# Expert weights asked for only after the second block, with the stage's own buffers first in the ring

## The chip, the cores and the metric

The kernel runs on one core of a Trainium2 chip. The metric is the device time of one execution in microseconds (us), median of 3 runs. The engines are TensorE (PE; PEld is its weight load), VectorE (DVE), ScalarE (ACT), GpSimd (POOL) and SyncE (SP). SP issues all DMAs of this kernel, in one queue and in the order of the program.

## The reference, cut to what matters

A first block of two layers works on 256 tokens of width 1024. A second block mixes a state-space branch (s5), a sparse attention and a memory attention, and ends in an output projection:

```python
merged = g_s * (y_ssm @ w_up_ssm) + g_d * (y_dsa @ w_up_dsa) + g_m * (y_mem @ w_up_mem)
x = x + merged @ w_out
x = x + hier_moe(rms_norm_2(x, g_ffn), w_group, b_group, w_expert, b_expert, w_gate, w_up, w_down)
```

`hier_moe` has 32 experts. A router (`w_group`, `w_expert`) picks two of them for each token. Gate, up and down weights of all 32 are read: each expert has 1024x512 gate, 1024x512 up and 512x1024 down, in fp32, 201 MB together.

## The kernel before

The experts run in 16 pairs. Each pair takes 24 pieces of weights of 128x1024 fp32, 512 KB each: 16 of gate and up, then 8 of down, 384 pieces in all. `fetch` (L1330) issues the DMA of the next piece on SP. It takes its buffer from `ring` (L1313), and a manual dependency keeps the pieces in their order of use on the queue. The first lap goes through the 35 letters of `RING` (L42), each one buffer: `e` two tiles of their own (`we`), `u` general tiles of the pool with 16 buffers that both blocks and the experts use (`unit`, L270), `x` four tiles of the pool `wx`, which lies where the second block's working tiles were, `w`, `h`, `l` the buffers of the split projection weights (`wraw`, `whi`, `wlo`), `T`, `t` those of transposed activations (`Thi`, `Tlo`), `b` one row buffer. Four more `u` tiles (`FIRST`) follow, then the laps repeat over the 35.

A piece's DMA waits on SP until the last user of its buffer is done, and everything behind it on SP waits with it. It also waits for one of eight completion semaphores (DMAHW0 to 7), which go round, so at most eight DMAs are under way.

Before the experts stands the second block. Its steps run in the order of the table `ORDER2` (L108 to 113), by `run_steps`. A step `name,args/k` sets `share`; a step without `/k` sets it back to the usual 4. The steps named here: `b,q,i` and `end,q` are the s5 blocks (L931 to L959), `glu` a projection behind them, `up,i,c` the three up projections (`up,0` is the last, w_up_ssm), `ahead,n` calls `fetch` n times. `ahead,2` at the top takes the two `we`; `ahead,6` at the end takes the six `u`.

Behind the table comes the output projection: the transposes (`tsplit`, L286 to L288), then `proj_tok` over eight weight pieces of w_out. Every projection weight is split by `wsplit` (L214): ACT makes `whi` (L216), and `wlo` (L217) comes from POOL for every `share`-th piece, otherwise from DVE:

```python
(G if share[0] and scount[0] % share[0] == 0 else V).tensor_sub(
```

`router_weights` (L1366) loads w_group and w_expert into a `u` tile, scales them (L1374) and splits them into a second `u` tile `wrs` (L1376, L1377). The first steps of the expert stage are the router: transposes of x, sixteen matmuls of `Thi` and `Tlo` with `wrs` (through L149), then some 6 us of small DVE work, then the one-hot gather (L1509) and the experts' matmuls, L1550 (gate, up) and L1572 (down). The program is ordered by a scheduler that follows data, buffers and priorities.

Of the kernel before, what the change touches and what calls it, by code (L numbers as in the profile page):

```python
# [38 lines left out]
HPR = 600  # L39

CAP = 64
RING = "e" * 2 + "u" * 6 + "x" * 4 + "w" * 5 + "h" * 5 + "l" * 4 + "T" * 4 + "t" * 4 + "b"  # L42

FIRST = 4

# [63 lines left out]
ahead,2 mn sa sp lo wm nt kv prep,0 u/6 b,0,1/1 keys/6 vk mem_q sel,0 queries/3 mem,0 b,0,0/3 gate,2,1/6 mem,1 b,0,3/1  # L109
gate,2,0/0 prep,1 up,2,0 up,2,1/0 b,1,0 sel,1 b,0,2/0 b,1,1/1 end,0 dsa,0 dsa,1 gate,1,1/0 b,1,2/2 b,1,3/1  # L110
prep,2 gate,1,0 up,1,0/6 up,1,1/3 b,2,0 end,1 prep,3 b,2,2/2 b,3,0 b,3,2 b,2,1/1 b,2,3/1 gate,0,1 gate,0,0
b,3,1/1 end,2 b,3,3/0 end,3 glu/2 up,0,1/2 up,0,0/2 ahead,6
"""
TWO_PI = 6.283185

# [6 lines left out]
def tile_model(ctx: ExitStack, tc: tile.TileContext, I: dict, out: bass.AP):  # L122
# [1190 lines left out]
    def ring():  # L1313

        n = turns[0]
        turns[0] += 1
        if n < len(RING):
            w = kinds[RING[n]]()
            slots.append(w)
            return w  # L1320
        if n < len(RING) + FIRST:
            return firsts.pop(0)
        return slots[(n - FIRST) % len(RING)]

# [413 lines left out]
```

## Time and profile before

| | |
|---|---|
| median of 3 runs | 1797.05 us (1796.57 to 1798.23) |
| the profiled execution | 1801.36 us, its span 1799.6 us |
| PE busy | 94%, mean granted clock 0.973 |
| DVE, ACT, POOL busy | 57%, 39%, 18% |
| DMA | 389.65 MB, 217 GB/s over the span, about 409 GB/s in the expert stage |
| first and second layer, second block | up to about 1318 us |
| experts | the rest, 1318 to 1799.6 us |

All times below are us from the start of the span of that one execution. PE's 94% is the busy share of pipelined matmuls, and does not say by itself that PE is the limit in the expert stage; the chain of waits and the DMA rate do.

### The profile page before, as it was taken

How to read it: one execution, taken by the hardware profiler on the slowest of the kernel's cores; microseconds unless marked ns; L12 is line 12 of the kernel's file. 1: busy time of each engine (PE TensorE's matmuls, PEld its weight loads, DVE VectorE, ACT ScalarE, POOL GpSimd, SP SyncE). 2: the span in 40 equal slices, each digit the busy share in tenths (PEclk: the TensorE clock that was granted, in tenths of full speed). 3: DMA queues.
4: the chain of work that ended last, by engine and by line, in shares of the span. 5: the costliest groups of instructions: out<-in, count | busy, mean ns of one | idle time of the engine just before them, and what ended most of it. 6: DMA issues, size and time to landing. Idle time of an engine off the chain costs nothing.

```text
span 1799.6 us, 24178 instructions
## 1 busy us (share of the span) xinstructions
PE 1688.6 (94%) x9005; PEld 1266.1 (70%) x9005; DVE 1025.9 (57%) x1659; ACT 708.2 (39%) x1345; POOL 318.4 (18%) x247
## 2 busy tenths in 40 slices
PE   7999999999999999999998998876879999999998
PEld 6899888888798999888877876765644444434342
DVE  6656656666673568675669899799631212212121
ACT  4455555644444656565546552421411010100000
POOL 0111106220102101321024343365100000000000
PEclk9999999999999999999999998987989999999999
DMA  8654445455566534453664633223699999999997
GB/s 261 188 142 137 140 145 144 148 166 164 164 174 178 171 111 141 135 164 102 197 190 149 180 106 111 66 70 107 196 378 369 410 409 408 409 409 409 409 409 297
DMA packets 186104, 389.65 MB, mean 217 GB/s; under 512 B 28736, under 2 KB 66816, under 8 KB 185984
## 3 DMA queue, kind: packets, MB, share of 16 engines
q1 hardware_dynamic: 185984, 388.08, 63.3%
q8 instruction: 72, 1.18, 0.3%
q14 instruction: 48, 0.39, 0.1%
HBM read 386.98 MB, written 1.05 MB: 216 GB/s over the span
## 4 chain that ended last, share of the span: by engine, by line
PE 70%; DMA 13%; DVE 11%; issue 2%; POOL 2%; ACT 1%; SPq 0%; DVEq 0%; POOLq 0%; ACTq 0%
PE proj L149 45%; PE proj L1550 7%; PE sc L149 5%; PE pv L149 4%; PE sc L1572 4%; DMA whi<-in_w_up_dram 2%; DMA Tlo<-in_w_up_dram 2%; DVE wlo L217 2%; PE tp L1509 1%; PE tp L365 1%; PE tp L286 1%; DMA wlo<-in_w_up_dram 1%; DMA wx<-in_w_up_dram 1%; DMA wraw<-in_w_down_dram 1%; DVE u L935 1%
## 5 line engine op out<-in xcount | busy, mean ns | idle before, releaser
L216 ACT CAST whi<-wraw 128x1024 fp32r<-128x1024 f32 x336 | 351.8, 1051 | 319.0 <-PE proj L149 263.1
L217 DVE TENSOR_TENSOR wlo<-wraw,whi 128x1024 fp32r<-128x1024 f32 (+1 forms) x287 | 376.7, 1316 | 172.0 <-PE proj L149 119.2
L149 PE MATMUL proj<-wlo,Thi 128*128 128x512 f32 (+1 forms) x1056 | 419.4, 397 | 6.2 <-DVE wlo L217 6.2
L149 PE MATMUL proj<-whi,Thi 128*128 128x512 f32 (+1 forms) x1056 | 419.4, 399 | 2.3 <-ACT P L988 1.0
L149 PE MATMUL proj<-whi,Tlo 128*128 128x512 f32 (+1 forms) x1056 | 415.7, 396 | 2.4 <-DVE Tlo L288 2.4
L149 PEld LDWEIGHTS proj<-wlo,Thi 128*128 128x128 f32 x1056 | 201.3, 191 | 48.3 <-DVE wlo L217 8.0
L149 PEld LDWEIGHTS proj<-whi,Thi 128*128 128x128 f32 x1056 | 201.4, 191 | 44.6 <-DVE u L1273 1.9
L149 PEld LDWEIGHTS proj<-whi,Tlo 128*128 128x128 f32 x1056 | 200.9, 190 | 43.1 <-DVE Tlo L288 2.9
L217 POOL TENSOR_TENSOR wlo<-wraw,whi 128x1024 fp32r<-128x1024 f32 (+1 forms) x49 | 125.4, 2559 | 434.4 <-PE proj L149 332.4
L149 PE MATMUL proj<-Thi,whi 128*128 128x256 f32 x576 | 165.2, 291 | 6.0 <-DVE u L468 3.0
L149 PE MATMUL proj<-Thi,wlo 128*128 128x256 f32 x576 | 165.8, 289 | 3.6 <-DVE wlo L217 3.6
L149 PE MATMUL proj<-Tlo,whi 128*128 128x256 f32 x576 | 164.8, 290 | 0.1
L1554 DVE SCALAR_TENSOR_TENSOR th<-th,cg,proj 128x512 f32<-128x512 f32 x16 | 12.0, 747 | 214.1 <-PE proj L1550 212.0
L149 PEld LDWEIGHTS proj<-Thi,whi 128*128 128x128 f32 x576 | 112.5, 197 | 7.8 <-DVE u L468 3.2
L149 PEld LDWEIGHTS proj<-Thi,wlo 128*128 128x128 f32 x576 | 113.5, 197 | 4.0 <-DVE wlo L217 3.8
L149 PEld LDWEIGHTS proj<-Tlo,whi 128*128 128x128 f32 x576 | 112.6, 197 | 0.4 <-DVE Tlo L959 0.3
L149 PE MATMUL sc<-u 128*128 128x256 f32 (+1 forms) x416 | 101.0, 359 | 11.8 <-DVE u L930 11.8
L1553 ACT ACTIVATE th<-proj,cg 128x512 f32<-128x512 f32 x16 | 11.0, 687 | 192.4 <-PE proj L1550 192.4
L149 PEld LDWEIGHTS sc<-u 128*128 128x128 f32 x416 | 70.6, 198 | 20.0 <-issue 11.9
L1576 DVE TENSOR_TENSOR u<-sc,u 128x512 fp32r<-128x512 f32 x32 | 22.0, 692 | 109.5 <-ACT u L1575 90.4
L356 ACT ACTIVATE P<-sc,nm 128x256 f32<-128x256 f32 (+1 forms) x152 | 63.7, 432 | 36.2 <-DVE nm L349 22.1
L1575 ACT CAST u<-sc 128x512 fp32r<-128x512 f32 x32 | 18.6, 585 | 136.1 <-PE sc L1572 122.0
(464 smaller groups left out, 2489.1 us busy)
## 6 DMA issues: line engine op xcount, KB each, us to landing
wraw<-in_w_in_dram SPq DMA_DIRECT2D x236, 512.0 KB, 3.8
wraw<-in_w_proj_dram SPq DMA_DIRECT2D x48, 512.0 KB, 4.3
u<-in_w_up_dram SPq DMA_DIRECT2D x25, 512.0 KB, 10.2
wraw<-in_w_out_dram SPq DMA_DIRECT2D x24, 512.0 KB, 4.4
u<-in_w_gate_dram SPq DMA_DIRECT2D x24, 512.0 KB, 10.2
wraw<-in_w_up_dram SPq DMA_DIRECT2D x21, 512.0 KB, 10.2
whi<-in_w_down_dram SPq DMA_DIRECT2D x21, 512.0 KB, 10.2
u<-in_w_down_dram SPq DMA_DIRECT2D x21, 512.0 KB, 10.1
```

Of the source, the lines that this page charges most:

```text
L149: T.matmul(o, l, r, start=start, stop=stop)
L216: S.copy(hi[:, :, :n], raw[:, :, :n])
L217: (G if share[0] and scount[0] % share[0] == 0 else V).tensor_sub(lo[:, :, :n], raw[:, :, :n], hi[:, :, :n].bitcast(F32))
L286: T.transpose(ps[:, b, :], src[:, b * 128:(b + 1) * 128], ident)
L356: S.activation(P[:, i * nS:(i + 1) * nS], scv[:, i, :], AF.Exp, bias=nm[:, i:i + 1], accum_out=l_out[:, i:i + 1])
L365: T.transpose(tp[:, j, :], P[:, j * 128:(j + 1) * 128], ident)
L935: V.tensor_tensor_scan(m[:, 256:512], rb, hi, 0.0, op0=OP.mult, op1=OP.add)
L1509: pin(T.matmul(tp[:, k, :], src[t][:, k0 + k, :], ohv[:, t], start=n == 0, stop=n == 3))
L1550: pin(T.matmul(ps[r], xk, w[:, 512 * j:512 * j + 512], start=k == 0, stop=k == 7))
L1572: pin(T.matmul(po[c][r], hT[:, k, r], w[:, 512 * c:512 * c + 512], start=k == 0, stop=k == 3))
L1575: S.copy(yh[:, c], po[c])
L1576: V.tensor_sub(yl[:, c], po[c], yh[:, c].bitcast(F32))
```

## The change

The step `ahead,6` at the end of `ORDER2` is gone, so no piece beyond the first two is asked for inside the second block. In `RING` the four `x` stand before the six `u`. Pieces 3 to 6 now go to `wx`, pieces 7 to 12 to `u` tiles, which are allocated only in the expert stage, behind the router's own tiles. Since the table now ends with `up,0,0/2`, `share` stays 2 and not 4 for the eight w_out pieces behind it: four of their `wlo` are made on POOL instead of two.

```diff
-RING = "e" * 2 + "u" * 6 + "x" * 4 + "w" * 5 + "h" * 5 + "l" * 4 + "T" * 4 + "t" * 4 + "b"
+RING = "e" * 2 + "x" * 4 + "u" * 6 + "w" * 5 + "h" * 5 + "l" * 4 + "T" * 4 + "t" * 4 + "b"
...
-b,3,1/1 end,2 b,3,3/0 end,3 glu/2 up,0,1/2 up,0,0/2 ahead,6
+b,3,1/1 end,2 b,3,3/0 end,3 glu/2 up,0,1/2 up,0,0/2
```

SP before, from the last w_out load on (`wraw_11799`), where ring pieces 13 to 16 follow directly; all six `u` pieces stand at least 13 rows further up:

```order
L1338 DMA wx_12115<-in_w_up_2_dram 128x1024 [waits DMAHW1_49]
L1338 DMA wx_12117<-in_w_up_2_dram 128x1024 [waits DMAHW2_49]
L201 DMA wraw_11793<-in_w_out_2_dram 128x2x512 [waits DMAHW3_49,DVE_49]
L201 DMA wraw_11799<-in_w_out_2_dram 128x2x512 [waits DMAHW4_49,DVE_49]
L1338 DMA wraw_12155<-in_w_gate_2_dram 128x1024 [waits DMAHW5_49,Pool_49]
L1338 DMA wraw_12157<-in_w_gate_2_dram 128x1024 [waits DMAHW6_49,DVE_49,Activation_49]
L1338 DMA wraw_12163<-in_w_up_2_dram 128x1024 [waits DMAHW7_49,DVE_49]
L1338 DMA wraw_12165<-in_w_up_2_dram 128x1024 [waits DMAHW3_49,DMAHW0_49,DVE_49]
```

SP now, from the last two w_out loads on:

```order
L201 DMA wraw_11781<-in_w_out_2_dram 128x2x512 [waits DMAHW5_49,Pool_49]
L201 DMA wraw_11787<-in_w_out_2_dram 128x2x512 [waits DMAHW6_49,DVE_49]
L1338 DMA u_12088<-in_w_up_2_dram 128x1024 [waits DMAHW7_49,PE_49]
L1338 DMA u_12090<-in_w_up_2_dram 128x1024 [waits DMAHW0_49]
L1338 DMA u_12107<-in_w_gate_2_dram 128x1024 [waits DMAHW1_49,PE_49]
L1338 DMA u_12109<-in_w_gate_2_dram 128x1024 [waits DMAHW2_49,DVE_49]
L1338 DMA u_12115<-in_w_up_2_dram 128x1024 [waits DMAHW3_49,PE_49]
L1338 DMA u_12117<-in_w_up_2_dram 128x1024 [waits DMAHW4_49,PE_49]
L1338 DMA wraw_12155<-in_w_gate_2_dram 128x1024 [waits DMAHW5_49,Pool_49]
L1338 DMA wraw_12157<-in_w_gate_2_dram 128x1024 [waits DMAHW6_49,DVE_49,Activation_49]
```

The six `u` pieces stand between the last w_out load and the rest of the ring. The sixth, `u_12117`, has the address of `u_11851`, which is `wrs`; the PE count that it waits for is that of the last router matmul that reads `wrs` (`proj_11935<-Thi_11896,u_11851`). Before, the first piece that waited for the same matmul was the 30th of the ring:

```order
L1336 DMA wlo_12209<-in_w_down_2_dram 128x1024 [waits DMAHW0_49]
L1338 DMA wlo_12226<-in_w_gate_2_dram 128x1024 [waits DMAHW1_49]
L1338 DMA wlo_12228<-in_w_gate_2_dram 128x1024 [waits DMAHW2_49]
L1338 DMA Thi_12234<-in_w_up_2_dram 128x1024 [waits DMAHW3_49]
L1338 DMA Thi_12236<-in_w_up_2_dram 128x1024 [waits DMAHW4_49]
L1338 DMA Thi_12242<-in_w_gate_2_dram 128x1024 [waits DMAHW5_49,DVE_49,PE_49]
L1338 DMA Thi_12244<-in_w_gate_2_dram 128x1024 [waits DMAHW6_49,DVE_49,PE_49]
L1338 DMA Tlo_12250<-in_w_up_2_dram 128x1024 [waits DMAHW7_49]
```

That is `Thi_12244`, whose buffer was the router's own operand. Now it is the twelfth.

DVE at the last two s5 blocks, before (-) and now (+); L936 to L940 and L950 to L959 are the s5 steps:

```order
 L952 TENSOR_TENSOR cva<-u 128x256
+L1374 TENSOR_TENSOR u<-u,g_11848 128x288
 L936 TENSOR_TENSOR u<-u 128x512
 L937 TENSOR_TENSOR u<-u 128x512
 L953 TENSOR_SCALAR cva<-cva 128x256
+L1377 TENSOR_TENSOR u<-u 128x8x36
 L939 TENSOR_TENSOR u<-u 128x256
 L940 TENSOR_TENSOR u<-u 128x256
 L954 TENSOR_TENSOR cva<-cva,u 128x256
+L950 SCALAR_TENSOR_TENSOR u<-u,s5d,pv 128x256
 L956 SCALAR_TENSOR_TENSOR u<-cva,u 128x256
-L950 SCALAR_TENSOR_TENSOR u<-u,s5d,pv 128x256
```

The two steps on the router's weights moved up into the last s5 block, since their loads now stand ahead of w_out's, and L950 stands before the L956 of the block ahead.

## Rows read from the trace of the kernel before

**Rows 1.** The page: GB/s moved in 40 slices of 45 us.

```profile
GB/s 261 188 142 137 140 145 144 148 166 164 164 174 178 171 111 141 135 164 102 197 190 149 180 106 111 66 70 107 196 378 369 410 409 408 409 409 409 409 409 297
```

**Rows 2.** Busy time by stretch; the first line names the columns.

```profile
core 0: us, PE busy (x) PEld busy (x) DVE busy (x) ACT busy (x) POOL busy (x), PEclk, DMA share, GB/s
...
1248.00:1264.00 16.00, 10.61 (x42) 8.82 (x42) 13.83 (x26) 1.67 (x4) 4.71 (x3) 0.79 0.95 330
1264.00:1284.00 20.00, 17.59 (x79) 13.77 (x79) 14.64 (x23) 10.48 (x18) 5.77 (x17) 0.91 0.65 220
1284.00:1296.00 12.00, 9.80 (x41) 8.09 (x42) 6.13 (x9) 2.54 (x5) 0.10 (x1) 0.86 0.28 91
1296.00:1318.20 22.20, 18.91 (x95) 15.23 (x93) 12.11 (x18) 10.64 (x17) 3.11 (x2) 0.96 0.82 265
1318.20:1352.00 33.80, 25.06 (x114) 12.40 (x114) 10.82 (x54) 3.55 (x7) 0.00 (x0) 0.77 1.03 410
1352.00:1364.00 12.00, 10.38 (x50) 3.77 (x50) 0.75 (x1) 0.58 (x1) 0.00 (x0) 1.00 1.00 349
...
1384.00:1392.00 8.00, 8.00 (x40) 2.75 (x38) 1.38 (x2) 1.17 (x2) 0.00 (x0) 1.00 0.86 265
```

**Rows 3.** SP's queue in order of time: start, length, what, count.

```profile
1248.57 1.13 SPq L1338 DMA_DIRECT2D u<-in_w_up_dram  x2
...
1277.55 7.80 SPq L201 DMA_DIRECT2D wraw<-in_w_out_dram  x2
1285.45 11.37 SPq L1338 DMA_DIRECT2D wraw<-in_w_gate_dram  x2
...
1318.20 0.33 SPq L1338 DMA_DIRECT2D Thi<-in_w_gate_dram  x1
...
1774.23 4.17 SPq L1336 DMA_DIRECT2D Thi<-in_w_down_dram  x4
```

**Rows 4.** Timeline of PE: the last router matmul.

```profile
1317.76 0.41 PE L149 MATMUL proj<-Thi,u 128*72 128x256 f32 x1
```

**Rows 5.** The chain that ended last: start, length, what, two of its links.

```profile
1550.81 10.18 DMA Thi<-in_w_up_dram
...
1643.63 10.18 DMA Tlo<-in_w_up_dram
```

**Rows 6.** The page, DMA issues: count, size, median us to landing.

```profile
wraw<-in_w_in_dram SPq DMA_DIRECT2D x236, 512.0 KB, 3.8
```

**Rows 7.** Timeline of DVE at the end of the s5 blocks and behind it.

```profile
1258.25 0.42 DVE L940 TENSOR_TENSOR u<-u 128x256 f32<-128x256 f32 x1
...
1259.48 0.43 DVE L956 SCALAR_TENSOR_TENSOR u<-cva,u 128x256 f32<-128x256 f32 x1 [0.48 <-ACT cva L955]
1260.56 0.48 DVE L950 SCALAR_TENSOR_TENSOR u<-u,s5d,pv 128x256 f32<-128x256 f32 x1 [0.66 <-PE pv L149]
...
1271.44 0.45 DVE L1374 TENSOR_TENSOR u<-u,g 128x288 f32<-128x288 f32 x1
...
1273.61 0.45 DVE L1377 TENSOR_TENSOR u<-u 128x288 fp32r<-128x288 f32 x1
```

**Rows 8.** Splits of w_out on DVE and POOL, and PE's wait behind them.

```profile
1281.28 2.59 POOL L217 TENSOR_TENSOR wlo<-wraw,whi 128x1024 fp32r<-128x1024 f32 x1
...
1281.55 3.40 DVE L217 TENSOR_TENSOR wlo<-wraw,whi 128x1024 fp32r<-128x1024 f32 x1
...
1295.19 1.23 DVE L217 TENSOR_TENSOR wlo<-wraw,whi 128x1024 fp32r<-128x1024 f32 x1 [0.67 <-PE proj L149]
...
1286.20 0.79 PE L149 MATMUL proj<-whi,Tlo 128*128 128x512 f32 x1 [2.44 <-DVE Tlo L288]
```

**Rows 9.** Timeline of PE: first matmuls of pair 0 on pieces in `wx` and `wraw`.

```profile
1342.38 3.65 PE L1550 MATMUL proj<-wx,u 128*64 128x512 f32 x16 [0.78 <-DVE u L1510]
...
1348.68 3.65 PE L1550 MATMUL proj<-wraw,u 128*64 128x512 f32 x16
```

## The prediction

> **What bounds the kernel now.** I read the page's bytes by slice first [rows 1]. From slice 30 on the rate stands at 408 to 410 GB/s until the last slice: the expert stage ends when its stream of 384 pieces ends. The chain of waits says the same from another side: in the second half it runs through DMAs, one link being a piece from issue to landing (10.18 us), after which the eighth piece behind it is issued [rows 5]. From 1550.81 to 1643.63 there are nine such links, so 92.82 us / 72 pieces = 1.289 us per piece. What happens to the time is therefore decided by one question: how many pieces are already under way when the stream can run without a break, and when that is.
>
> Then I followed SP's queue back to the start of the stream [rows 3]. Six `u` pieces go out from 1248.57 on. The last w_out load leaves just before 1285.45, the next ring pieces wait for `wraw` buffers, and from 1296 to 1318.2 the queue already moves 265 GB/s [rows 2]. The 30th piece (`Thi`) goes out at 1318.20 [rows 3], in the instant in which the last router matmul ends (1317.76 + 0.41 = 1318.17) [rows 4]. So 29 pieces were issued before the router was done. Nothing after that holds the stream for long: two dips, 349 GB/s over 12 us and 265 over 8 us, when the ring is full and PE must free buffers [rows 2].
>
> **The change part by part.** *The new wait.* The six `u` pieces now stand behind the last w_out load. Five of them find free tiles; the stretch 1284 to 1296 has room for them (91 GB/s, DMA share 0.28) [rows 2]. The sixth, piece 12, has the buffer of the router's split weights and waits for the router's last matmul. SP is one queue, and in it all other pieces stand behind piece 12: the `wraw`, `whi` and `wlo` pieces, the first of which went out from 1285.45 to 1315 before, are held too. Where 29 pieces were out at the router's end, 11 will be. That is 18 pieces of 1.289 us, 23 us of stream, of which a part was under way and not landed, and a part was lost again in the two dips. I don't sum these; I time the end of the stream directly.
>
> Call T the time at which the router's last matmul ends. Piece 12 is issued at T. It goes into an empty queue, and lands after the median of such a load, 3.8 us [rows 6]. Seven more are issued right behind it, and piece 20 when piece 12 has landed. From there one piece follows every 1.289 us. The first of the last four `Thi` pieces is the 381st, 361 behind the 20th: T + 3.8 + 361 x 1.289 = T + 469.1. Before it was issued at 1774.23 [rows 3]. The page gives 3.8 for a 512 KB load. The Trainium skill, "DMA: Bandwidth & Descriptors", section "Anatomy of one DMA", fits 2.0 us + bytes / 436 GB/s for the other issue path, an estimate of 3.2 us here; by it the sum would be 0.6 us less, and no run here shows that figure.
>
> With T unchanged at 1318.17 the 381st goes out at 1787.3, 13.0 us later than before. The tail behind it does not change: eight down pieces, their matmuls, the scatter and the store. PE is no hindrance at the start of the stage: the last of pair 0's gate and up pieces, the 16th, lands at about T + 3.8 + 4 x 1.289 = 1327, and PE came to the `wraw` pieces only at 1348.68 [rows 9]. The dips fall away, since the ring is no longer full at that time; they are in the old 1774.23 and not in the new sum, so their gain is already counted.
>
> *What moves T.* Before T stand the end of the s5 blocks, glu, w_up_ssm and w_out.
> (a) L1374 and L1377 move from behind the s5 blocks into the last one, 0.45 us each [rows 7]. DVE has no gap there up to L940, and PE waits for that result, so 0.9 us is added. In their old places nobody waited for them.
> (b) L956 of the third block now comes after L950 of the fourth; its 0.43 us was hidden in DVE's wait for PE, and is now in front of the fourth's chain [rows 7]: +0.4.
> (c) The w_out loads no longer share the DMA with six `u` pieces (330 GB/s from 1248 to 1264) [rows 2]. In the list of waits no engine waits for a w_out piece there, so this gives 0.
> (d) Four splits on POOL and not two. A POOL split is 2.59 us, and a DVE split that ran beside it took 3.40 us, against 1.23 us for one without a neighbour [rows 8]. The first such pair, at 1281, exists before and now, and PE waits 2.44 us behind it both times. The second half of w_out gets one more pair; there PE runs from 1286 on nearly without a gap, and the splits come well ahead of their matmuls. I take 0; uncovered it would be 3.40 - 1.23 = 2.2.
> T = 1318.2 + 0.9 + 0.4 = 1319.5.
>
> T has two ends. Early: the wait of 2.44 us goes, and with it the lower clock behind it, an estimate from the row for 1284 to 1296 of 9.80 x (1 - 0.86) = 1.4 us [rows 2, 8]; T = 1318.2 - 3.8 = 1314.4. Late: (a), (b) and an uncovered (d); T = 1319.5 + 2.2 = 1321.7.
>
> *The sum.* 381st piece at 1319.5 + 469.1 = 1788.6; before 1774.23; the span grows by 14.4 us, from 1799.6 to 1814.0. The profiled execution took 1801.36 us, 4.3 above the median of the runs. I add the difference to the median: 1797.05 + 14.4 = **1811.4 us**, 0.8% slower.
>
> **The rivals.**
> *Not slower: the wait does not bind.* The place is piece 12 on SP. If its buffer were free with the other five, all six would go out in the gap from 1284 to 1296, where 0.72 x 12 = 8.6 us of DMA time lies idle for 6 x 1.289 = 7.7 us of pieces, and the ring would go on as before, with w_out's loads earlier. The price would be about nothing, 1797. The point from which it decides: T + 469.1 = 1774.23, so piece 12 must leave before 1305.1. For this speaks the gap that is there. Against it: the wait in the built program names the router's matmul, the 30th piece, which waited for the same one, went out in the very instant that it ended [rows 3, 4], and T can't come 13 us sooner: PE's idle time from 1264 to 1318.2 is only 2.4 + 2.2 + 3.3 = 7.9 us [rows 2]. Chance 0.08, 0.05 of it within 0.2% and 0.03 faster.
> *Slower, but less.* PE's wait before the w_out matmuls goes since DVE's order changed around it; T = 1314.4, the 381st at 1783.5, 1797.05 + 9.3 = 1806.3. For it: POOL takes the second w_out split, which stood on DVE ahead of the last sums of the up projection. Against it: the pair that made the wait is still there. Chance 0.12.
> *Slower by more: DVE and POOL hold each other up.* The row shows a DVE split 2.2 us longer beside a POOL split [rows 8]. If the added pair has no cover, T = 1321.7 and the time is 1813.6. The Trainium skill, "SBUF — State Buffer", section "SBUF: two separate sides", says that DVE with two SBUF inputs and a reading GpSimd operation exclude each other for a whole instruction; the row agrees, since 1281.28 + 2.59 + 1.23 = 1285.1 is near the DVE split's end at 1284.95. Chance 0.10, since PE had slack there.
> *The forecast*, T near 1319.5 and a stream of 1.289 us per piece: 0.70.
>
> **How the numbers follow.** A difference of 0.2% (3.6 us) is about what a measurement of this kernel can tell from no change. Forecast 0.70, less 0.12, more 0.10: slower 0.92; same 0.05; faster 0.03. The price of a piece has an end of its own: links of 10.18 us without the small gaps between some of them give about 1.28, which takes off 361 x 0.009 = 3.3 us. The range goes from the early T (1806.3) less some of that, 1805.0, to the late T (1813.6) and the 1.7 us by which the runs of before differ, 1815.3. It leaves out the rival in which the wait does not bind.
>
> **What would show it.** In the profile after: the SP queue issues five `u` pieces between about 1285 and 1292 and the sixth right behind the last router matmul, with `wraw<-in_w_gate` behind it; the DMA rate from 1296 to T near zero, then 410 GB/s with no dips near 1352 and 1384; the chain of waits turning to DMAs earlier in the expert stage than before; the last four `Thi` issues near 1788.6; the router's end near 1319.5. If piece 12 leaves before the router ends, or the rate between 1296 and 1318 stays at 265 GB/s, the prediction is wrong at its root. If T lies outside 1314 to 1322, the sum is off by that much, and in particular by (a), (b) or (d).

## The result

The changed kernel takes 1806.53 us (median of 5 runs, 1804.39 to 1807.44) beside 1797.05 for the one before (5 runs, 1795.76 to 1798.23): 9.5 us more, ratio 1.0052, 95% interval 1.0037 to 1.0067. It is slower, as forecast, by 9.5 us and not by 14.4.

The mechanism that the prediction names is there. SP's queue in the changed kernel (start, length, what; the answer to [rows 3]):

```profile
1277.38 0.90 SPq L1338 DMA_DIRECT2D u<-in_w_up_dram  x2
1278.36 1.67 SPq L1338 DMA_DIRECT2D u<-in_w_gate_dram  x2
1282.15 26.31 SPq L1338 DMA_DIRECT2D u<-in_w_up_dram  x2
1308.55 0.86 SPq L1338 DMA_DIRECT2D wraw<-in_w_gate_dram  x2
...
1778.32 4.17 SPq L1336 DMA_DIRECT2D Thi<-in_w_down_dram  x4
```

Five `u` pieces go out up to 1282.15. The row "x2" of 26.31 us holds the fifth and the sixth: the sixth, the 12th piece of the ring, leaves at 1308.13 (1282.15 + 26.31 less the 0.33 of its own issue), and the `wraw` pieces stand behind it. The router's last matmul in the changed kernel ends at 1307.82 + 0.28 = 1308.10:

```profile
1307.82 0.28 PE L149 MATMUL proj<-Thi,u 128*72 128x256 f32 x1
```

The stretches show the same silence (columns and order as in [rows 2], cut at the matching places):

```profile
1243.20:1259.20 16.00, 10.31 (x41) 8.69 (x41) 14.28 (x27) 2.10 (x5) 5.29 (x11) 0.79 0.62 169
1259.20:1279.20 20.00, 17.40 (x83) 13.32 (x84) 15.47 (x23) 10.21 (x17) 8.47 (x11) 1.00 0.59 204
1279.20:1291.20 12.00, 12.00 (x60) 10.01 (x60) 7.73 (x8) 6.37 (x9) 3.07 (x2) 1.00 0.65 245
1291.20:1308.10 16.90, 13.64 (x73) 10.98 (x71) 8.52 (x15) 6.81 (x12) 3.32 (x2) 1.00 0.00 0
1308.10:1339.00 30.90, 22.13 (x105) 11.65 (x106) 10.63 (x53) 2.31 (x6) 0.00 (x0) 0.78 0.98 375
1339.00:1380.00 41.00, 38.69 (x200) 16.64 (x198) 8.72 (x20) 6.08 (x11) 0.00 (x0) 1.00 1.03 409
```

In the 16.9 us before the router's end nothing moves, where it was 265 GB/s. Behind it the queue first fills (375 GB/s over 31 us), and then there is no dip any more: 409 GB/s from 1339 on. In the page's slices (45 us each, against [rows 1]) the row is flat from there to the last:

```profile
GB/s 270 193 137 146 126 162 128 140 187 160 145 198 191 148 120 126 135 175 101 210 196 140 171 104 104 47 83 105 122 387 409 409 409 409 409 409 409 409 409 298
```

The chain of waits turns to the transfers at 1452.90, where it was 1540.60 before, with the same link as in [rows 5]:

```profile
1449.40 3.50 PE sc L1572 x15
1452.90 10.15 DMA whi<-in_w_up_dram
```

**Reading the two traces side by side.** The profiled spans differ by only 5.0 us (1799.6 and 1804.6), less than the medians. The code up to the s5 blocks is the same in both, and yet the same instructions stand 4.6 us apart at 50 us (53.57 and 48.96) and 4.8 us apart at 1215. DVE before, a line of the start and one ahead of the changed stretch:

```profile
53.57 1.00 DVE L511 SCALAR_TENSOR_TENSOR cva<-proj,cw,cva 128x255 f32<-128x255 f32 x2 [1.66 <-ACT cva L509]
...
1218.79 0.68 DVE L929 TENSOR_TENSOR u<-sc,u 128x512 f32<-128x512 f32 x1
```

DVE after, the same two:

```profile
48.96 1.00 DVE L511 SCALAR_TENSOR_TENSOR cva<-proj,cw,cva 128x255 f32<-128x255 f32 x2 [0.22 <-ACT cva L509]
...
1214.01 0.68 DVE L929 TENSOR_TENSOR u<-sc,u 128x512 f32<-128x512 f32 x1
```

So the profiled execution of before had lost 4.6 us within its first 55 us, where the two programs are the same, and 4.8 us ahead of the changed stretch. It is the odd one: in the seven traces of the experiments below the first line stands between 48.7 and 50.7 us, the second between 1211.7 and 1213.6. It fits that this execution took 4.3 us more than the median of its kernel. Below, "aligned" means a time of before less 4.8. Aligned, the effect of the change on the span is 1804.6 - (1799.6 - 4.8) = 9.8 us, as the medians say. It splits into three: the router's end, T, comes at 1308.13 instead of 1318.2 - 4.8 = 1313.4, **5.3 us earlier**; from T to the 381st piece it takes 1778.32 - 1308.13 = 470.2 instead of 1774.23 - 1318.2 = 456.0, **14.2 us longer**; the tail takes 26.3 instead of 25.4, 0.9 longer. -5.3 + 14.2 + 0.9 = 9.8.

### The profile page after: what moved, and what is told of

It is laid out like the page before. It is cut to its first block, busy times and chain, and to the rows that moved or that the text cites. A ratio compares the mean times of both kernels' runs of the same rounds, so it can differ in the third digit from the quotient of the medians.

```text
span 1804.6 us, 24172 instructions
## 1 busy us (share of the span) xinstructions
PE 1695.5 (94%) x9005; PEld 1262.8 (70%) x9005; DVE 1025.9 (57%) x1657; ACT 708.5 (39%) x1345; POOL 323.9 (18%) x249
## 4 chain that ended last, share of the span: by engine, by line
PE 67%; DMA 17%; DVE 10%; POOL 2%; issue 2%; ACT 1%; SPq 0%; DVEq 0%; POOLq 0%; ACTq 0%
PE proj L149 46%; PE sc L149 5%; PE proj L1550 4%; PE pv L149 4%; DMA whi<-in_w_up_dram 3%; DMA u<-in_w_up_dram 3%; PE sc L1572 3%; DVE wlo L217 2%; DMA wraw<-in_w_down_dram 2%; DMA Tlo<-in_w_up_dram 2%; PE tp L365 1%; PE tp L286 1%; DMA wraw<-in_w_up_dram 1%; DMA wlo<-in_w_up_dram 1%; DMA Thi<-in_w_up_dram 1%
## 5 line engine op out<-in xcount | busy, mean ns | idle before, releaser
L217 POOL TENSOR_TENSOR wlo<-wraw,whi 128x1024 fp32r<-128x1024 f32 (+1 forms) x51 | 131.8, 2585 | 424.2 <-PE proj L149 308.0
L149 PEld LDWEIGHTS sc<-u 128*128 128x128 f32 x416 | 70.2, 197 | 22.4 <-issue 14.4
```

Source lines behind the costliest of these rows:

```text
L149: T.matmul(o, l, r, start=start, stop=stop)
```

## The experiments

Two questions were left: is the held piece the whole loss, and does the number of pieces behind it set its size; and why does the router end 5.3 us earlier, where I forecast 1.3 later. All times are medians; experiments 1 to 4 ran beside runs of before with a median of 1795.39 us (29 runs), 5 to 7 beside 1795.69 (17 runs). The ratios are not the quotients of these medians but lie up to 0.14% above them, so a difference to the kernel before is known to within some 2.5 us. Differences below are those of the medians.

| run | us | ratio to before, 95% |
|---|---|---|
| 1: changed, ring in the old order | 1790.97 | 0.9985 (0.9973 to 0.9998) |
| 2: changed, five `u` pieces | 1792.07 | 0.9990 (0.9979 to 1.0000) |
| 3: changed, share of splits as elsewhere | 1806.64 | 1.0074 (1.0057 to 1.0092) |
| 4: before, share of splits as in the changed one | 1795.34 | 1.0002 (0.9989 to 1.0015) |
| 5: before, `ones` without a load | 1790.61 | 0.9977 (0.9967 to 0.9988) |
| 6: changed, held piece is the 17th | 1798.60 | 1.0030 (1.0017 to 1.0043) |
| 7: changed, held piece is the 10th | 1809.27 | 1.0082 (1.0068 to 1.0097) |

**1. Only the early request is taken away.**

```diff
-RING = "e" * 2 + "x" * 4 + "u" * 6 + "w" * 5 + "h" * 5 + "l" * 4 + "T" * 4 + "t" * 4 + "b"
+RING = "e" * 2 + "u" * 6 + "x" * 4 + "w" * 5 + "h" * 5 + "l" * 4 + "T" * 4 + "t" * 4 + "b"
```

(- is the changed kernel.)

> The changed kernel with the ring in its old order (u pieces before the wx pieces); only the six early pieces are left out. In this order the gather's second operand, and not a u piece, gets the buffer of the router's split weights, so no piece of the ring waits for the router before the first Thi piece that needs the router's halves, the 30th. Main theory (the whole loss is the 12th piece waiting on SP for the router's last matmul): nothing but the order on SP's queue differs from the changed kernel; 29 pieces are out when the router ends, as before the change, and the router ends 5.3 us earlier than before as in the changed kernel (1318.2 - 4.8 against 1308.1, times aligned), so 1797.05 - 5.3 = about 1792 us, and at most 1797. Rival (what costs is that the six pieces are asked for later, behind w_out's loads): as the changed kernel, 1806.5 us.

Measured 1790.97 us, 15.6 less than the changed kernel (15.7 less than experiment 3, which ran beside it and has the changed ring) and 4.4 less than the one before (2.7 by the ratio). SP's queue in this run:

```profile
1281.38 1.70 SPq L1338 DMA_DIRECT2D wx<-in_w_up_dram  x2
1284.13 1.63 SPq L1338 DMA_DIRECT2D wraw<-in_w_gate_dram  x2
...
1304.63 1.73 SPq L1338 DMA_DIRECT2D Thi<-in_w_gate_dram  x2
...
1759.90 4.18 SPq L1336 DMA_DIRECT2D Thi<-in_w_down_dram  x4
```

All six `u` pieces, the `wx` and the `wraw` go out before the router ends; the 30th piece, the second of the `Thi` row, leaves at 1306.03 and is again the one that waits for it (the last router matmul ends at 1306.00). From there to the 381st it takes 1759.90 - 1306.03 = 453.9 us, where it was 456.0 before the change. So the half of the change that asks for nothing ahead costs nothing. The loss comes from the other half, the `wx` pieces in front: they shift the rotation of the `u` buffers by one, and give a ring piece the buffer of the router's weights that otherwise the gather takes. In the built program of this run the address of `wrs` (`u_11851`) goes to the gather's `u_12096`; in the changed kernel it goes to `u_12117`, the sixth `u` piece.

**2. The held piece alone is taken away.**

```diff
-RING = "e" * 2 + "x" * 4 + "u" * 6 + "w" * 5 + "h" * 5 + "l" * 4 + "T" * 4 + "t" * 4 + "b"
+RING = "e" * 2 + "x" * 4 + "u" * 5 + "w" * 5 + "h" * 5 + "l" * 4 + "T" * 4 + "t" * 4 + "b"
```

> The changed kernel, order of the ring kept, with five u pieces instead of six, so that the piece which waited for the router's split weights is not there; the ring is one piece shorter. Main theory: 27 to 28 pieces are out at the router's end instead of 11, no silence on the DMA queue before 1308, the 381st piece is no later than about 1771 in the times of the changed kernel, total about 1792 + at most 1.3 us for the slot that is missing when the ring is full = 1792 to 1794 us. Rival (a later request for the ring as such, or wx ahead of u as such): 1806 us or more.

Measured 1792.07 us. `wx` stays in front, 28 pieces are out when the router ends at 1308.16, and the loss is gone all the same. It is 1.1 us above experiment 1; I expected up to 1.3 for the missing slot, but the intervals of the two ratios overlap, so this part is not settled.

**3 and 4. The share of splits.** The last step of the order table sets the share that w_out inherits. Without the `ahead,6` one split in two goes to POOL, with it one in four. Experiment 3 sets the changed kernel back to one in four, experiment 4 gives the kernel before one in two.

```diff
-b,3,1/1 end,2 b,3,3/0 end,3 glu/2 up,0,1/2 up,0,0/2
+b,3,1/1 end,2 b,3,3/0 end,3 glu/2 up,0,1/2 up,0,0/2 ahead,0
```

```diff
-b,3,1/1 end,2 b,3,3/0 end,3 glu/2 up,0,1/2 up,0,0/2 ahead,6
+b,3,1/1 end,2 b,3,3/0 end,3 glu/2 up,0,1/2 up,0,0/2 ahead,6/2
```

> The changed kernel with the share of weight splits that go to POOL in w_out set back to one in four, as the usual share is; before it was one in two only because the last step of the order table sets it. Two of w_out's splits on POOL and not four; nothing else differs. The router ended 5.3 us earlier in the changed kernel than in the one before, where I had forecast 1.3 later. Theory A (it is the splits: with four on POOL the DVE queue ahead of w_out is shorter and PE's wait of 2.44 us goes): PE waits again for a DVE split before w_out, the router ends 3.8 to 6.6 us later, 1810 to 1813 us. Theory B (the early router comes from the order around the s5 blocks, or from the DMA queue free of ring pieces): 1806.5 us within 1.

> The kernel before, with one in two of w_out's splits on POOL instead of one in four; the six early pieces and the ring's order stay. Theory A (the splits on POOL bring the early router): the router ends 3.8 to 5.3 us earlier, and since 29 pieces are out at that time the stream of the experts begins and ends as much earlier: 1792 to 1793 us. Theory B (the early router of the changed kernel has another cause): 1797 us within 1; if the added splits on POOL hold DVE up in turn, up to 1799.

Measured 1806.64 and 1795.34 us, each as its own kernel without the edit (1806.53 and 1795.39): Theory A falls in both directions. The ratio of experiment 3 (1.0074) is larger than that of the changed kernel (1.0052), but their intervals overlap. The early router comes with the changed kernel whatever the share is. The rows say what differs. Experiment 4, first DVE, then POOL (start, length, engine, line, what):

```profile
1273.78 0.23 DVE L1393 TENSOR_SCALAR ones<-upper_f 128x128 fp32r<-128x128 f32 x1 [0.92 <-DMA upper_f<-in_c_upper_dram]
...
1276.33 3.39 DVE L217 TENSOR_TENSOR wlo<-wraw,whi 128x1024 fp32r<-128x1024 f32 x1
```

```profile
1276.05 2.59 POOL L217 TENSOR_TENSOR wlo<-wraw,whi 128x1024 fp32r<-128x1024 f32 x1
```

Experiment 3, the same two splits:

```profile
1275.39 1.22 DVE L217 TENSOR_TENSOR wlo<-wraw,whi 128x1024 fp32r<-128x1024 f32 x1
```

```profile
1275.55 3.30 POOL L217 TENSOR_TENSOR wlo<-wraw,whi 128x1024 fp32r<-128x1024 f32 x1 [8.87 <-PE proj L149]
```

In each pair the split that starts second is the one that is held, and which starts second goes with the kernel, not with the share. In experiment 4, as before, DVE comes late because L1393 waits for a load.

**5. That load is taken off DVE's path in the kernel before.** Its row in the kernel before, on DVE, ahead of the 3.40 us split of [rows 8]:

```profile
1277.02 1.28 DVE L1273 SCALAR_TENSOR_TENSOR u<-u,proj 128x512 f32<-128x512 f32 x2
1279.01 0.23 DVE L1393 TENSOR_SCALAR ones<-upper_f 128x128 fp32r<-128x128 f32 x1 [0.71 <-DMA upper_f<-in_c_upper_dram]
1279.15 0.68 DVE L1273 SCALAR_TENSOR_TENSOR u<-u,proj 128x512 f32<-128x512 f32 x1
1279.75 1.89 DVE L1274 TENSOR_TENSOR u<-u 128x512 f32<-128x512 f32 x3
```

SP's queue before: the load stands behind two ring pieces.

```profile
1271.91 0.81 SPq L1338 DMA_DIRECT2D wx<-in_w_gate_dram  x2
1272.82 0.38 SPq L1390 DMA_DIRECT2D upper_f<-in_c_upper_dram  x1
```

From 1272.82 to its landing it takes 6.2 us. In the changed kernel it is issued at 1267.13, no ring piece is in flight, and it takes 2.6 us. The edit gives L1393 another source of the same shape, of which it uses only the size (times 0, plus 1):

```diff
-        V.tensor_scalar(ones, upper_f, 0.0, 1.0, op0=OP.mult, op1=OP.add)
+        V.tensor_scalar(ones, ident, 0.0, 1.0, op0=OP.mult, op1=OP.add)
```

> The kernel before, with one source changed: L1393 makes its tile of ones from the identity, which is there from the start, and not from the matrix whose load (L1390) DVE waited for in the kernel before at 1279.01, with two ring pieces in front of that load. Six early pieces, ring and splits stay. In the kernel before DVE stood 0.71 us there, its w_out split started at 1281.55 behind POOL's at 1281.28 and took 3.40 us; in the changed kernel the load is alone, DVE does not wait, its split starts first (1275.67 against 1275.83) and takes 1.22. Theory C (that wait made DVE late, so that POOL's split held DVE's up, PE waited 2.44 us and its clock fell): DVE's split starts at about 1280.5 in the times of before, ahead of POOL's, takes 1.2 us, PE's wait of 2.44 goes, the router ends 3.8 to 5 us earlier, total 1790.5 to 1792 us beside 1795.4. Theory D (the order of the two splits comes from POOL's queue, where a memset in front of the split waits for DVE): POOL's split still starts first, 1795 us within 1.

Measured 1790.61 us, 5.1 less than before (4.1 by the ratio). DVE in this run:

```profile
1272.87 1.88 DVE L1273 SCALAR_TENSOR_TENSOR u<-u,proj 128x512 f32<-128x512 f32 x3
1274.66 1.89 DVE L1274 TENSOR_TENSOR u<-u 128x512 f32<-128x512 f32 x3
1276.47 1.22 DVE L217 TENSOR_TENSOR wlo<-wraw,whi 128x1024 fp32r<-128x1024 f32 x1
```

and POOL:

```profile
1276.01 0.10 POOL L274 MEMSET u<- 128x1 f32 x1 [6.92 <-DVE u L1274]
1276.67 3.25 POOL L217 TENSOR_TENSOR wlo<-wraw,whi 128x1024 fp32r<-128x1024 f32 x1 [0.56 <-PE proj L149]
```

DVE's split starts 0.2 us ahead of POOL's and takes 1.22 us. In the list of waits PE's longest wait for this result falls from 2.4 us to 1.1, before and in this run:

```profile
PE proj L149 <- DVE Tlo L288: 3.6, 2, 2.4
```

```profile
PE proj L149 <- DVE Tlo L288: 1.1, 1, 1.1
```

The memset of Theory D still stands in front of POOL's split, but it has left by 1276.1, and the split then waits for PE. Theory C holds.

All nine traces say the same. I take a matmul of `glu` ahead of the splits as the start; before, and after:

```profile
1265.54 0.58 PE L149 MATMUL proj<-Thi,whi 128*128 128x256 f32 x1 [0.30 <-ACT cva L967]
```

```profile
1260.88 0.39 PE L149 MATMUL proj<-Thi,whi 128*128 128x256 f32 x1 [0.30 <-ACT cva L967]
```

From it to the end of the router's last matmul it takes 52.6 us in the kernel before and in experiment 4, the two in which POOL's split starts first. In the other seven DVE's split starts first, by 0.15 to 0.20 us, and it takes 47.2 to 47.9 us.

The kernel of experiment 5, with all six early pieces, is as fast as experiment 1 without them: the early pieces gain nothing even so, and in the kernel before they cost 4 to 5 us by way of this one load.

**6 and 7. How many pieces are out.** The ring's order is changed so that the held piece is the 17th, or the 10th.

```diff
-RING = "e" * 2 + "x" * 4 + "u" * 6 + "w" * 5 + "h" * 5 + "l" * 4 + "T" * 4 + "t" * 4 + "b"
+RING = "e" * 2 + "x" * 4 + "w" * 5 + "u" * 6 + "h" * 5 + "l" * 4 + "T" * 4 + "t" * 4 + "b"
```

```diff
-RING = "e" * 2 + "x" * 4 + "u" * 6 + "w" * 5 + "h" * 5 + "l" * 4 + "T" * 4 + "t" * 4 + "b"
+RING = "e" * 2 + "x" * 2 + "u" * 6 + "x" * 2 + "w" * 5 + "h" * 5 + "l" * 4 + "T" * 4 + "t" * 4 + "b"
```

> The changed kernel with the u pieces behind the five wraw pieces: the piece that waits for the router's split weights is now the 17th of the ring and not the 12th; everything else is the same. Main theory (the end of the stream is the router's end + 4.5 us + 1.289 us for each piece behind the eight that go out at the router's end): five pieces more are out at the router's end, so the 381st goes out 5 x 1.289 = 6.4 us earlier, 1806.5 - 6.4 = about 1800 us. Rival (only whether the queue is held counts, not how many pieces are out): 1806.5 us within 1.

> The changed kernel with two of the wx pieces put behind the u pieces: the piece that waits for the router's split weights is the 10th of the ring and not the 12th. Main theory: two pieces fewer are out at the router's end, the 381st goes out 2 x 1.289 = 2.6 us later, 1806.5 + 2.6 = about 1809 us. Rival (how many pieces are out does not count): 1806.5 us within 1.

Measured 1798.60 and 1809.27 us, on 1800 and 1809 forecast. SP's queue of experiment 6:

```profile
1307.42 0.33 SPq L1336 DMA_DIRECT2D u<-in_w_down_dram  x1
1307.80 2.62 SPq L1336 DMA_DIRECT2D whi<-in_w_down_dram  x5
...
1770.80 4.17 SPq L1336 DMA_DIRECT2D Thi<-in_w_down_dram  x4
```

and of experiment 7, where the held piece, the second of the first row, leaves at 1282.24 + 27.02 - 0.33 = 1308.93:

```profile
1282.24 27.02 SPq L1338 DMA_DIRECT2D u<-in_w_gate_dram  x2
1309.31 0.90 SPq L1338 DMA_DIRECT2D wx<-in_w_up_dram  x2
...
1781.86 4.17 SPq L1336 DMA_DIRECT2D Thi<-in_w_down_dram  x4
```

From the held piece to the 381st: 1770.80 - 1307.42 = 463.4 with 16 pieces out, 470.2 with 11, 1781.86 - 1308.93 = 472.9 with 9. That is 6.8 us for five pieces and 2.7 for two, about 1.36 each, where the link gave 1.289. It does not go on like this up to the 29 pieces of before: there it is 456.0, so that 18 pieces are worth 14.2 us, 0.8 each. Some of the 29 had not landed when the router ended, and that stream lost time in the two dips of [rows 2]; how much is due to each isn't measured.

## Why the prediction was right, and where it was off

**Piece 12 waits for the router: right.** Five `u` pieces out, the sixth at T, the `wraw` pieces behind it, no transfer before T, no dips after: all rows are there, and experiments 1 and 2 show that without this one wait the loss is gone. I did not say which half of the change makes the wait: it is the order of the ring, not the missing early request.

**The stream's term: right.** I gave T + 469.1 for the 381st piece; it is T + 470.2. The 12th piece landed 4.5 us after its issue, not 3.8 (the 20th goes out at 1312.64); that is 0.7 of the 1.1. From the 20th to the 381st it takes 1778.32 - 1312.64 = 465.7 us, 1.290 for each piece. Experiments 6 and 7 confirm the term in its dose. The tail, which I left unchanged, is 0.9 us longer. One reading in front of the sum was loose: in [rows 1] the rate stands at 408 to 410 GB/s only from the 32nd slice on; the 30th and 31st have 378 and 369.

**The term T: wrong by 6.6 us.** I had it 1.3 us later; aligned it is 5.3 earlier, at 1312.9, outside the 1314 to 1322 that I gave as a sign of being wrong. By its parts:

(a) and (b), +0.9 and +0.4: together they cost 0.1 us. The rows of DVE after, which answer to [rows 7]:

```profile
1251.70 0.45 DVE L1374 TENSOR_TENSOR u<-u,g 128x288 f32<-128x288 f32 x1
...
1253.48 0.45 DVE L1377 TENSOR_TENSOR u<-u 128x288 fp32r<-128x288 f32 x1
...
1255.68 0.48 DVE L950 SCALAR_TENSOR_TENSOR u<-u,s5d,pv 128x256 f32<-128x256 f32 x1 [0.74 <-PE pv L149]
```

The two steps are where I put them, 0.45 us each, but L950 stands at 1255.68 against 1260.56 - 4.8 = 1255.76. It waits for PE (0.74 us, before 0.66), so PE's matmuls set it and not DVE's queue. The line "PE waits for that result" is where (a) failed: there was slack that I had not read. (b) failed in the same way. L956 now runs behind L950, at 1256.07, where I put it, but the `glu` matmul shown under experiment 5, behind the whole s5 stretch, stands at 1260.88 against 1265.54 - 4.8 = 1260.74.

(c), 0: this is the step that failed. I looked only for waits on w_out's pieces. The load that mattered was another that shared the queue, the small one of L1390, for which DVE waited 0.71 us. This is too short to count by itself; what it cost is the order behind it.

(d), 0 for the added splits: right, as experiments 3 and 4 show. But under it I wrote that the first pair of splits "exists before and now, and PE waits 2.44 us behind it both times". The pair is there; its order turned. DVE after, the stretch of [rows 8]:

```profile
1269.75 0.23 DVE L1393 TENSOR_SCALAR ones<-upper_f 128x128 fp32r<-128x128 f32 x1 [1.34 <-DMA upper_f<-in_c_upper_dram]
1272.06 1.88 DVE L1273 SCALAR_TENSOR_TENSOR u<-u,proj 128x512 f32<-128x512 f32 x3 [2.09 <-PE proj L149]
...
1275.67 1.22 DVE L217 TENSOR_TENSOR wlo<-wraw,whi 128x1024 fp32r<-128x1024 f32 x1
```

and POOL:

```profile
1275.83 3.29 POOL L217 TENSOR_TENSOR wlo<-wraw,whi 128x1024 fp32r<-128x1024 f32 x1 [1.85 <-PE proj L149]
```

L1393 now waits where nothing else is due. The three sums of L1273 run without a gap, the split starts 1.1 us earlier (1275.67 against 1281.55 - 4.8 = 1276.75), ahead of POOL's, and PE does not wait the 2.44 us.

How the 5.3 us divide: from 1264 to 1318.2 PE was busy 17.59 + 9.80 + 18.91 = 46.3 us at granted clocks of 0.91, 0.86 and 0.96 [rows 2]; after, 17.40 + 12.00 + 13.64 = 43.0 us at 1.00, the full level of 2.4 GHz, in all three stretches. That is 3.3 us of busy time; idle time falls from 7.9 to 5.9, 2.0 us. The kernel before has two dips of the clock in this stretch (columns as in [rows 2]):

```profile
1266.00:1269.00 3.00, 3.00 (x15) 2.86 (x15) 1.35 (x4) 1.76 (x4) 0.51 (x1) 0.54 0.53 160
...
1287.00:1290.00 3.00, 3.00 (x9) 2.34 (x9) 0.35 (x1) 0.00 (x0) 0.00 (x0) 0.62 0.86 315
```

The second stands behind the wait (PE is busy for 0.80 us from 1284 to 1287) and goes with it: experiment 5, which has no such wait, has 1.00 from 1258 to 1309. Experiment 4 keeps the wait and has a dip behind it too, 0.71 and 0.72 from 1280 to 1286. For the first dip I have no cause, and it is no part of the price: experiment 4 does not have it (1.00 from 1258 to 1280) and takes the same 52.6 us, since PE there waits 1.6 us for another DVE result. So experiment 4 shows the price of the wait alone. From the `glu` matmul to the router's end PE is busy 43.6 us there and 41.7 in the changed kernel, and idle 9.0 and 5.5 us: of the 5.3 us, 3.4 are waits and 1.9 are the clock.

**The rivals.** The time (1806.53) fits the rival "slower, but less" (1806.3), which I gave a chance of 0.12, better than the forecast of 1811.4. Its mechanism was the right one, the wait and the clock behind it that go away, but its reason was not: I let POOL's extra split clear the way, and experiments 3 and 4 exclude that. That the two times agree to 0.2 us is partly luck: it had T 3.8 us earlier and not 5.3, and the 1.1 us of the stream and the 0.9 us of the tail make up for that. The range took the time in at its low end because this rival had set that end. "Slower by more" did not come: DVE and POOL do hold each other up, but with DVE first it is POOL that pays, and in the list of waits of the changed kernel PE waits for no result of POOL there. "Not slower" failed as its own test said: it needed T before 1305.1, and T came at 1308.1, or 1312.9 on the clock of before.

## What to carry to other kernels

In a queue that issues in order, look up for each transfer whose buffer it takes over: one that waits for a late reader holds every transfer behind it. With few pieces out each held one cost about a piece's time (1.36 us); all 18 together cost less than 18 pieces (14.2 us), so the end of the stream has to be timed and not the pieces counted. Changing the order in which buffers are taken from a rotating pool can move such waits to other transfers, so the new pairs have to be read, not the old ones. And when a stream moves away from a stretch, ask which small loads there had stood behind it and who waited for them: a wait of 0.7 us can decide which of two engines starts first, and so several microseconds.

## What the runs showed of the hardware

Of two splits of 128x1024 that overlap on DVE and POOL, the one that starts second is held: with POOL 0.27 us ahead, POOL takes 2.59 us and DVE 3.40; with DVE 0.15 to 0.20 us ahead, DVE takes 1.22 (1.23 alone) and POOL 3.25 to 3.31 (2.40 alone). The Trainium skill, "SBUF — State Buffer", section "SBUF: two separate sides", says that of a DVE operation with two SBUF inputs and a GpSimd operation that reads SBUF, whichever starts first has the shared ports for its whole instruction while the other is blocked. These rows agree, but for the 0.19 us that POOL's split is longer when it is first. In this kernel a start of DVE's split 0.4 us earlier against POOL's was enough to move the cost from one engine to the other.

The 64 KB load of L1390, issued right behind two ring pieces, lands after 6.2, 7.0 and 6.4 us (the kernel before, experiments 4 and 5), and after 2.1 to 2.6 us in the six traces in which no ring piece is in flight. And identical code at the start of the program stood 4.6 us apart in two executions, half of what this change does: traces have to be aligned at an instruction ahead of the change before they are subtracted.
